# Attention scores computed from unsplit fp32 operands, with four smaller moves, in a one-core macaron block (RWKV-7 plus sliding-window attention)

## The chip, the core and the metric

The kernel runs on one core of a Trainium2 chip. The core has five engines that run side by side, each through its own list of instructions in order: TensorE (PE; its weight loads are listed as PEld), VectorE (DVE), ScalarE (ACT), GpSimd (POOL) and SyncE (SP), which here only issues DMAs. Matmuls write to PSUM; everything else lies in SBUF. The metric is the device time of one execution in microseconds, as the median of several runs.

## The reference, cut to what matters

One layer on x of 512 rows by 1024 columns, all in fp32:

```python
x = x + 0.5 * swiglu(rms_norm(x, norm_ffn1), ffn1_gate, ffn1_up, ffn1_down)   # 1024 -> 2816 -> 1024
p = rms_norm(x, norm_mix) @ w_in
o_rwkv = rwkv7_time_mix(p[..., :1792], ...)                 # 8 heads of 64, recurrent over rows
q, k, v = split(p[..., 1792:] + b_in_attn)                  # 8 query heads, 2 key/value heads of 64
scores = einsum('bnqhgd,bnkhd->bnhgqk', qb, kb) * 64 ** -0.5 # blocks of 128 rows, own and previous block
probs = softmax(concat([masked scores, sink]))[..., :-1]
out = einsum('bnhgqk,bnkhd->bnqhgd', probs, vb)
x = x + concat([o_rwkv, out]) @ w_out
x = x + 0.5 * swiglu(rms_norm(x, norm_ffn2), ffn2_gate, ffn2_up, ffn2_down)
return rms_norm(x, norm_final)
```

## The kernel before, in words

The program has five parts in a row: the first feed-forward net (`ffn("a")`), the input projections of the mixer, a joint stretch of recurrence and attention, the output projection (`out_mix`), and the second net (`ffn("b")`). In the nets and the projections PE issues matmuls without a pause to speak of. The large products are made in fp32r (names hi and lo): each operand is split into hi (rounded by ACT) and lo (the rest, by DVE), and three matmuls, hi·hi, lo·hi and hi·lo (`mm3w`, L683 to L685), give one product.

**Start.** `start` (L334) loads x in half rows (256 KB each) and the first weights over SP's queue: half row 0, the first two weight transfers (`a.loads(1)`), half rows 1 to 3, further weights. PE transposes each half row (xta), DVE scales it (xga), ACT and DVE split it (AaM).

**Plain stretch.** The last 256 hidden columns of a net are computed first, by `plain_step`, in four steps; at the fourth (L655) ACT and DVE make the results (gta, L658 and L659) and each is entered in the list `due`, with the step behind which PE transposes it (`hidden_turn`: hta on PE, hTa on ACT). Before, result t is due at step q + 1 + t, so the first transpose stands on PE behind the first of two X steps (L683 to L685, names Xa), 12 matmuls each.

**Join.** After the projections `join` (L1112) puts the inverse of the recurrence's triangle together: TT<-TB and held<-py on ACT and DVE, then on PE the product px, then TT<-px. The function `beside` puts other work between: the projection of v (`in_ps_av`), `split_k` and `split_q`, which make hi and lo of keys (ks, kl) and queries (qs), and the scores of unit 0. A unit is one block of 128 rows with one key/value head, four query heads; there are eight.

**Recurrence and attention.** What follows stands in a table written by hand (`ORDER`); its steps set the order on all engines. z is the product pz (eight matmuls) of a chunk, zd its copy by ACT (pack<-pz), u the product pu, sc the scores of a unit, m and w its maximum (DVE) and exponentials (ACT), t the transpose of the weights (pT) and te its copy (PT), a the product with v (av), wo the output projection. In `scores` (L1458) the two units of the first block multiply fp32 queries and keys directly, four matmuls over 64 rows and 128 columns. The six other units make two fp32r matmuls per head: queries' hi over lo, 128 rows deep, against ks, then queries' hi against kl, 64 rows deep, both with 256 columns. x, spilled to memory before, comes back by four DMAs that POOL issues (`unspill`, step ux); step var has POOL compute the power for a norm.

Of the kernel before, what the change touches and what calls it, by code (L numbers as in the profile page):

```python
# [53 lines left out]
gb.0 ud.2 s.2 w.4.1 m.6.0 o.2 a.2 n.2.0 oe.2 v.3 ah.2 we.4 te.3 n.2.1 z.3 m.6.1 wa.4.0 b.4 ve.3 al.2 sc.5 wd.4.1 zd.3  # L54
w.6.0 u.3 m.5.0 a.3 w.6.1 uv.3 t.4 m.5.1 ah.3 ud.3 s.3 we.6 te.4 al.3 o.3 n.3.0 sc.7 w.5.0 n.3.1 z.4 wa.6.0 m.7.0 b.5
w.5.1 wd.6.1 a.4 m.7.1 zd.4 t.6 oe.3 we.5 ah.4 wd.5.1 w.7.0 u.4 al.4 bp.1 uv.4 te.6 g.1 wd.5.0 w.7.1 bo.1 t.5 ud.4
we.7 s.4 wd.7.0 te.5 o.4 wd.7.1 a.6 oe.4 n.4.0 ge.1 a.5 n.4.1 ah.6 q.1 t.7 al.6 ah.5 b.6 wh.0 gb.1 z.5 al.5 te.7 var.1 ux
wl.0 q.0 a.7 zd.5 var.0 u.5 ah.7 wo.1.0 wh.1 al.7 uv.5 ns.1 s.5 ud.5 wl.1 ht.1 o.5 wo.1.1 n.5.0 oe.5 q.2 n.5.1 z.6 mg.1
b.7 wo.3.0 zd.6 var.2 xa.1 u.6 ns.0 wo.3.1 uv.6 ns.2 ud.6 s.6 xa.3 mh.1 o.6 n.6.0 ht.0 oe.6 ht.2 n.6.1 wo.0.0 mg.2 z.7
mg.0 mh.2 wo.0.1 zd.7 ml.2 mh.0 u.7 ml.1 wh.2 wo.2.0 xa.0 ud.7 wl.2 o.7 wo.2.1 oe.7 ml.0 q.3 wo.5.0 var.3 wh.3 xa.2  # L60
wl.3 wo.5.1 wo.4.0 xa.5 ns.3 wo.7.0 ht.3 wo.4.1 mg.3 wo.7.1 wh.4 xa.4 mh.3 wl.4 wo.6.0 ml.3 wo.6.1 xa.7 xa.6
# [121 lines left out]
class Net:  # L183
# [152 lines left out]
    def start(self, x):  # L336

        nc = self.nc
        self.warm()
        self.consts()  # L340
        xin = self.xin = self.new_rows()
        def load(h, *ts):
            for t in ts:
                nc.sync.dma_start(xin[t][:, h * S:h * S + S], x[0, t * P:(t + 1) * P, h * S:h * S + S])
        a = self.a = self.stream("a")
        load(0, 0)
        a.loads(1)
        load(0, 1, 2, 3)
        a.loads(2)
        load(1, 0, 1, 2, 3)  # L350
        a.loads(4)
        self.first_gain()
        self.ss = self.small("ss_a", 8, "ss")
        self.operands_begin("a")
        for t in range(2):
            self.start_turn(t, 0)
            if t == 0:
                a.split(0)
# [64 lines left out]
    def want_high(self, i):  # L423

        name, srcs = self.plan.pop(0)
        raw, n = self.weights_load(name, srcs)
        hi, lo = (self.wp.tile([P, 8, P], F32R, tag="o" + x, name=f"{x}_{name}", bufs=OUTW) for x in ("hi", "lo"))
        self.nc.scalar.activation(hi, raw, AF.Copy)
        self.half = name, raw, hi, lo

    def want_low(self, i):
        name, raw, hi, lo = self.half
# [13 lines left out]
    def weights(self, name, srcs):  # L446

        raw, n = self.weights_load(name, srcs)
        if name.startswith("be"):
            hi, lo = (self.tile4(f"{c}_{name}", (P, 8, P), F32R) for c in ("hi", "lo"))  # L450
        else:
            if name[0] == "o":
                hi, lo = (self.wp.tile([P, 8, P], F32R, tag="o" + x, name=f"{x}_{name}", bufs=OUTW) for x in ("hi", "lo"))
            else:
                hi, lo = (r.next(P) for r in self.split_rings)
        return self.weights_split(raw, n, hi, lo)
# [178 lines left out]
    def plain_step(self, st, pc):  # L635

        nc = self.nc
        if pc.idx == 0:
            self.banks["P"] = [self.acc(f"P{st.tag}{t}") for t in range(4)]
        bh, bl = st.parts[pc.q]  # L640
        for t in range(4):
            if pc.idx == 0 and t == 1 and st.tag == "a":
                for u in (2, 3):
                    self.operand_turn(self.xin[u], u, 0, self.gain1)
                for u in (2, 3):
                    self.operand_split(P_OPERANDS[1][0], u % 2)
            if pc.idx == 0 and t == 2 and st.tag == "b":
                self.out_turn(7)
            hi, lo = self.A[P_OPERANDS[t // 2][pc.idx // 2]]
            ts = slice(t % 2 * P, t % 2 * P + P)  # L650
            for j in range(2):
                k = 2 * (pc.idx % 2) + j
                self.mm3w(self.banks["P"][t], hi[:, k, ts], lo[:, k, ts], bh[:, j], bl[:, j], pc.idx == 0 and j == 0, pc.idx == 3 and j == 1)
        if pc.idx == 3:
            for t, b in enumerate(self.banks.pop("P")):  # L655
                ms = self.ms[:, t:t + 1]
                g, h = self.gt(f"pg{st.tag}{t}")[:, :256], self.gt(f"ph{st.tag}{t}")[:, :256]
                nc.scalar.activation(g, b[:, 256:], AF.Silu, scale=ms)  # L658
                nc.vector.scalar_tensor_tensor(h, b[:, :256], ms, g, ALU.mult, ALU.mult)  # L659
                self.due.append((pc.q + 1 + t, lambda t=t, h=h: self.hidden_turn(st, 5, t, h, 256)))  # L660

    def gu_step(self, st, pc):
        nc = self.nc
# [352 lines left out]
    def prep(self, p):  # L1016
        nc = self.nc
        k, r, a, Pd, Pi = self.kT[p], self.rT[p], self.icl[p], self.Pd[p], self.Pi[p]
        c3 = lambda t: t.rearrange("p (c t) -> p c t", c=NC)
        KR = self.KR[p] = self.tile4(f"KR{p}", (P, NC, 2, C))  # L1020
        BK = self.BK[p] = self.tile4(f"BK{p}", (P, NC, 2, C))
        STo = self.STo[p] = self.tile4(f"STo{p}", (P, NC, 2, C))
        kk = self.tile2(f"kk{p}")
        kk3 = c3(kk)
        nc.vector.scalar_tensor_tensor(kk, k, self.v("rwkv_k_k", p), self.knb[p].rearrange("p t s -> p (t s)"), ALU.mult, ALU.mult)
        nc.vector.tensor_tensor(KR[:, :, 1], c3(r), Pd, ALU.mult)
        nc.vector.tensor_tensor(KR[:, :, 0, 1:], kk3[:, :, 1:], Pd[:, :, :C - 1], ALU.mult)
        nc.vector.tensor_copy(KR[:, :, 0, 0], kk3[:, :, 0])
        nc.vector.tensor_tensor(kk, kk, a, ALU.mult)
        nc.scalar.activation(a, a, AF.Identity, scale=self.v("rwkv_k_a", p), bias=self.oka[:, p:p + 1])  # L1030
        nc.scalar.activation(STo[0:64], KR[64:128], AF.Copy)
        nc.vector.tensor_tensor(BK[:, :, 0], kk3, Pi, ALU.mult)
        nc.vector.tensor_tensor(k, k, a, ALU.mult)
        nc.vector.tensor_tensor(BK[:, :, 1], c3(k), Pi, ALU.mult)
# [124 lines left out]
    def gate(self, p):  # L1159

        nc = self.nc
        if p // 2 not in self.g:
            self.g[p // 2] = self.tile4(f"g{p // 2}")
        pt = self.gps[p] = self.psum(f"g_ps{p}")
        nc.tensor.matmul(pt, self.g2[:, p * P:(p + 1) * P], self.gl, start=True, stop=True)

# [7 lines left out]
    def mixer(self):  # L1174
# [55 lines left out]
        with self.tc.manual_schedule(engines=MAN):  # L1230
# [5 lines left out]
            def beside(i):  # L1236
                if i == 0:
                    part(0, 4)
                    self.split_k()
                    for n in range(1, 4):  # L1240
                        self.split_q(n)
                elif i == 1:
                    self.scores_all(0)
                    part(4, 8)
# [176 lines left out]
    def attn_begin(self):  # L1421
        nc = self.nc
        self.amix = self.pairs("am")
        self.sc, self.qs, self.PT, self.pp = {}, {}, {}, {}

    def attn_values(self):
        self.avn = self.psum("avn", (P, 4, P))
# [4 lines left out]
        self.Vn = self.keep("V", "Vn").rearrange("p (n c) -> p n c", n=4)  # L1432
        self.nc.scalar.activation(self.Vn, self.avn, AF.Copy)

    def split_k(self):

        nc = self.nc
        self.ks = self.x4.tile([P, 2, S], F32R, tag="ks", name="ks", bufs=1)
        self.kl = self.tile2("kl", dt=F32R) if "a" not in KEEP else self.t4.tile([P, 2, S], F32R, tag="kl", name="kl", bufs=1)[:, 0]
        for h in range(2):  # L1440
            r, o = (slice(x * 64, x * 64 + 64) for x in (h, 1 - h))
            nc.scalar.activation(self.ks[r, h], self.k[r], AF.Copy)
            nc.vector.tensor_tensor(self.kl[r], self.k[r], self.ks[r, h].bitcast(F32), ALU.subtract)
            nc.gpsimd.dma_start(self.ks[o, h], self.ks[r, h])

    def split_q(self, n):

        nc = self.nc
        qs = self.qs[n] = self.wp.tile([P, 2, 4, P], F32R, tag="qs", name=f"qs{n}", bufs=3)
        for i in range(2):  # L1450
            js = slice(2 * i, 2 * i + 2)
            for h in range(2):
                r, o = (slice(x * 64, x * 64 + 64) for x in (h, 1 - h))
                q, hi = self.q[i][r, :, n * P:(n + 1) * P], qs[r, h, js]
                nc.scalar.activation(hi, q, AF.Copy)
                nc.vector.tensor_tensor(qs[o, h, js], q, hi.bitcast(F32), ALU.subtract)

    def scores(self, u):  # L1458
        nc = self.nc
        n, h = u // 2, u % 2  # L1460
# [3 lines left out]
        pss = self.psum2(f"sc{u}", (P, 4, 2 * P))  # L1464
        for j in range(4):
            ks = slice((n - 1) * P + k0, (n + 1) * P)
            if n == 0:
                nc.tensor.matmul(pss[:, j, :W], self.q[j // 2][r0:r0 + 64, j % 2, :P], self.k[r0:r0 + 64, ks], start=True, stop=True)
            else:
                q = self.qs[n][:, h, j]  # L1470
                nc.tensor.matmul(pss[:, j, :W], q, self.ks[:, h, ks], start=True, stop=False)
                nc.tensor.matmul(pss[:, j, :W], q[r0:r0 + 64], self.kl[r0:r0 + 64, ks], start=False, stop=True)
        self.sc[u] = (self.extra4("sc", f"scs{u}", (P, 4, 2 * P)), W, pss) + tuple(self.small(f"{x}{u}", 4, x) for x in ("m", "nm", "es", "den"))

    def scores_max(self, u, half):
# [178 lines left out]
```

## Time and profile before

| | |
|---|---|
| median of 3 runs | 1001.09 us (999.86 to 1001.99) |
| profiled execution | 1002.43 us, its span 1000.7 us |
| PE busy | 976.9 us, 98% |
| DVE, ACT, POOL busy | 651.7, 502.9, 88.5 us |
| mean granted clock of PE | 0.988 |

The busy time of PE is modelled and contains the tail of each matmul, so 98% says that PE rarely stands, not that it works at its peak. A granted clock of 1.00 is 2.4 GHz, 0.50 is 1.2 GHz. The rows quoted below are of four kinds: sums of what PE waited for; busy time, clock and DMA share in chosen stretches; instructions in order of time (start in us, duration in us, engine, line, operation, output<-input, partitions x columns, count; in brackets the idle time of the engine before it and what ended it); and groups of equal instructions.

### The profile page before, as it was taken

How to read it: one execution, taken by the hardware profiler on the slowest of the kernel's cores; microseconds unless marked ns; L12 is line 12 of the kernel's file. 1: busy time of each engine (PE TensorE's matmuls, PEld its weight loads, DVE VectorE, ACT ScalarE, POOL GpSimd, SP SyncE). 2: the span in 40 equal slices, each digit the busy share in tenths (PEclk: the TensorE clock that was granted, in tenths of full speed). 3: DMA queues.
4: the chain of work that ended last, by engine and by line, in shares of the span. 5: the costliest groups of instructions: out<-in, count | busy, mean ns of one | idle time of the engine just before them, and what ended most of it. 6: DMA issues, size and time to landing. Idle time of an engine off the chain costs nothing.

```text
span 1000.7 us, 12967 instructions
## 1 busy us (share of the span) xinstructions
PE 976.9 (98%) x5041; PEld 794.6 (79%) x5041; DVE 651.7 (65%) x926; ACT 502.9 (50%) x777; POOL 88.5 (9%) x97
## 2 busy tenths in 40 slices
PE   8799999999999999999989999999999999999996
PEld 6688888888888886788876777887888888888885
DVE  5677667677522548699985687668767668753422
ACT  4655546546521327755466664265554654652302
POOL 0110010110000001120010030101010111000001
PEclk9899999999999999999999899999999999999999
DMA  9474855945332044223110253655594584533202
GB/s 316 106 168 113 225 135 122 232 105 182 111 104 84 12 103 140 75 74 73 43 33 23 52 152 132 226 156 147 124 234 110 143 202 97 206 126 115 75 1 84
DMA packets 83621, 124.09 MB, mean 124 GB/s; under 512 B 12772, under 2 KB 33320, under 8 KB 83560
## 3 DMA queue, kind: packets, MB, share of 16 engines
q1 hardware_dynamic: 67048, 89.17, 27.7%
q0 software_dynamic: 13856, 31.46, 15.8%
q10 hardware_dynamic: 2656, 2.63, 0.9%
q8 instruction: 39, 0.64, 0.3%
q14 instruction: 22, 0.18, 0.1%
HBM read 114.60 MB, written 6.29 MB: 121 GB/s over the span
## 4 chain that ended last, share of the span: by engine, by line
PE 85%; DVE 6%; ACT 4%; issue 2%; DMA 1%; POOL 1%; SPq 0%; POOLq 0%; ACTq 0%; DVEq 0%
PE da L685 4%; PE da L683 4%; PE db L685 4%; PE db L683 4%; PE da L684 4%; PE db L684 4%; PE Xa L685 4%; PE Xa L683 4%; PE Xa L684 4%; PE Xb L685 3%; PE Xb L683 3%; PE Xb L684 3%; PE Qb L685 2%; PE Qa L685 2%; PE Qa L683 2%
## 5 line engine op out<-in xcount | busy, mean ns | idle before, releaser
L160 ACT ACTIVATE hib<-rawa1b 128x1024 fp32r<-128x1024 f32 x38 | 40.2, 1057 | 58.4 <-PE db L684 19.4
L683 PE MATMUL da<-hia,dda 128*128 128x512 f32 x176 | 69.3, 394 | 0.0
L683 PE MATMUL db<-hib,ddb 128*128 128x512 f32 x176 | 68.8, 391 | 0.0
L685 PE MATMUL da<-loa,dda 128*128 128x512 f32 x176 | 68.6, 390 | 0.0
L684 PE MATMUL da<-hia,dda 128*128 128x512 f32 x176 | 68.5, 389 | 0.0
L685 PE MATMUL db<-lob,ddb 128*128 128x512 f32 x176 | 68.5, 389 | 0.0
L684 PE MATMUL db<-hib,ddb 128*128 128x512 f32 x176 | 68.5, 389 | 0.0
L160 ACT ACTIVATE hia<-rawa1a 128x1024 fp32r<-128x1024 f32 x38 | 40.1, 1055 | 49.6 <-DMA rawa1a<-in_ffn_gate_dram 17.6
L169 DVE TENSOR_TENSOR lob<-rawa1b,hib 128x1024 fp32r<-128x1024 f32 x38 | 46.4, 1220 | 28.3 <-PE db L685 22.6
L169 DVE TENSOR_TENSOR lob<-rawa0b,hib 128x1024 fp32r<-128x1024 f32 x38 | 46.4, 1220 | 28.3 <-PE db L685 21.7
L683 PE MATMUL Xa<-hia,AaM 128*128 128x512 f32 x160 | 64.0, 400 | 0.0
L685 PE MATMUL Xa<-loa,AaM 128*128 128x512 f32 x160 | 63.1, 395 | 0.9 <-DVE loa L169 0.9
L685 PE MATMUL Xb<-lob,AbM 128*128 128x512 f32 x160 | 62.6, 392 | 1.3 <-DVE lob L169 1.3
L683 PE MATMUL Xb<-hib,AbM 128*128 128x512 f32 x160 | 63.2, 395 | 0.0
L684 PE MATMUL Xa<-hia,AaM 128*128 128x512 f32 x160 | 62.8, 393 | 0.0
L684 PE MATMUL Xb<-hib,AbM 128*128 128x512 f32 x160 | 62.3, 390 | 0.0
L169 DVE TENSOR_TENSOR loa<-rawa0a,hia 128x1024 fp32r<-128x1024 f32 x38 | 46.4, 1220 | 20.9 <-PE da L685 14.6
L169 DVE TENSOR_TENSOR loa<-rawa1a,hia 128x1024 fp32r<-128x1024 f32 x38 | 46.4, 1220 | 15.8 <-PE da L685 8.8
L160 ACT ACTIVATE hib<-rawa0b 128x1024 fp32r<-128x1024 f32 x38 | 40.1, 1057 | 24.5 <-PE db L684 12.1
L160 ACT ACTIVATE hia<-rawa0a 128x1024 fp32r<-128x1024 f32 x38 | 40.1, 1055 | 15.4 <-PE da L684 11.2
L685 PEld LDWEIGHTS da<-loa,dda 128*128 128x128 f32 x176 | 33.0, 188 | 7.0
L685 PEld LDWEIGHTS db<-lob,ddb 128*128 128x128 f32 x176 | 33.0, 188 | 6.9
(460 smaller groups left out, 2527.9 us busy)
## 6 DMA issues: line engine op xcount, KB each, us to landing
rawa0a<-in_w_in_dram SPq DMA_DIRECT2D x16, 512.0 KB
rawa0a<-in_ffn_down_dram SPq DMA_DIRECT2D x11, 512.0 KB
rawa1a<-in_ffn_down_dram SPq DMA_DIRECT2D x11, 512.0 KB
rawa0b<-in_ffn_down_dram SPq DMA_DIRECT2D x11, 512.0 KB
rawa1b<-in_ffn_down_dram SPq DMA_DIRECT2D x11, 512.0 KB
rawba<-in_ffn_up_dram SPq DMA_DIRECT2D x10, 512.0 KB
rawba<-in_ffn_gate_dram SPq DMA_DIRECT2D x10, 512.0 KB
rawa0a<-in_ffn_gate_dram POOLq DMA_DIRECT2D x10, 512.0 KB, 5.9
```

Source lines behind the costliest of these rows:

```text
L160: self.nc.scalar.activation(hi, raw, AF.Copy)
L169: self.nc.vector.tensor_tensor(lo, raw, hi.bitcast(F32), ALU.subtract)
L683: mm(ps, ah, bh, start=first, stop=False, skip_group_check=True)
L684: mm(ps, al, bh, start=False, stop=False, skip_group_check=True)
L685: mm(ps, ah, bl, start=False, stop=last, skip_group_check=True)
```

## The change

1. **Scores.** `split_k` and `split_q` are gone. All eight units multiply the fp32 queries and keys: one matmul per head where two fp32r ones were. 
2. **Plain stretch.** Each transpose of a result is due one step later, in both nets. The eight result buffers are taken from their ring in another order, all gates first.
3. **First weights.** The first two weight transfers are issued from ACT's queue in place of SP's.
4. **Reload.** ux stands behind var.0 in the table in place of before it.
5. **Buffers.** KR and STo of a head pair, the two gate buffers, and hi and lo of each output weight each become one tile; the numbers of these buffers are as before or fall in with them, the first two move from one pool to another.

```diff
-we.7 s.4 ... al.5 te.7 var.1 ux
-wl.0 q.0 a.7 zd.5 var.0 u.5 ah.7 ...
+we.7 s.4 ... al.5 te.7 var.1
+wl.0 q.0 a.7 zd.5 var.0 ux u.5 ah.7 ...
...
-        a.loads(1)
+        a.loads(1, nc.scalar)
...
-        hi, lo = (self.wp.tile([P, 8, P], F32R, tag="o" + x, name=f"{x}_{name}", bufs=OUTW) for x in ("hi", "lo"))
+        hi, lo = self.out_pair(name)
...
+    def out_pair(self, name):
+        t = self.wp.tile([P, 2, 8, P], F32R, tag="ow", name="w_" + name, bufs=OUTW)
+        return t[:, 0], t[:, 1]
...
+            g4, h4 = ([self.gt(f"p{x}{st.tag}{t}")[:, :256] for t in range(4)] for x in "gh")
...
-                g, h = self.gt(f"pg{st.tag}{t}")[:, :256], self.gt(f"ph{st.tag}{t}")[:, :256]
+                g, h = g4[t], h4[t]
...
-                self.due.append((pc.q + 1 + t, lambda t=t, h=h: self.hidden_turn(st, 5, t, h, 256)))
+                self.due.append((pc.q + 2 + t, lambda t=t, h=h: self.hidden_turn(st, 5, t, h, 256)))
...
-        KR = self.KR[p] = self.tile4(f"KR{p}", (P, NC, 2, C))
-        STo = self.STo[p] = self.tile4(f"STo{p}", (P, NC, 2, C))
+        both = self.t8.tile([P, 2, NC, 2, C], F32, tag="KS", name=f"KS{p}", bufs=4)
+        KR, STo = self.KR[p], self.STo[p] = both[:, 0], both[:, 1]
...
-            self.g[p // 2] = self.tile4(f"g{p // 2}")
+            both = self.t8.tile([P, 2, 2, S], F32, tag="g", name="g", bufs=1)
+            self.g = {i: both[:, i] for i in range(2)}
...
                 if i == 0:
                     part(0, 4)
-                    self.split_k()
-                    for n in range(1, 4):
-                        self.split_q(n)
...
-            if n == 0:
-                nc.tensor.matmul(pss[:, j, :W], self.q[j // 2][r0:r0 + 64, j % 2, :P], self.k[r0:r0 + 64, ks], start=True, stop=True)
-            else:
-                q = self.qs[n][:, h, j]
-                nc.tensor.matmul(pss[:, j, :W], q, self.ks[:, h, ks], start=True, stop=False)
-                nc.tensor.matmul(pss[:, j, :W], q[r0:r0 + 64], self.kl[r0:r0 + 64, ks], start=False, stop=True)
+            nc.tensor.matmul(pss[:, j, :W], self.q[j // 2][r0:r0 + 64, j % 2, n * P:(n + 1) * P], self.k[r0:r0 + 64, ks], start=True, stop=True)
```

What this does to the lists of the engines is shown at three places. On ACT at the join, before; qs is the split of the queries for blocks 1 to 3, TT and held the moves of the join, held<-in_ps_av the copy of v, scs the exponentials:

```order
L1110 ACTIVATE TT<-TB 32x2x8x32 x4
L1110 ACTIVATE held<-py 128x256
L1442 ACTIVATE ks<-held 64x512 x2
L1455 ACTIVATE qs_3684<-q_2361 64x256 x2
L1455 ACTIVATE qs_3684<-q_2362 64x256 x2
L1455 ACTIVATE qs_3693<-q_2361 64x256 x2
L1455 ACTIVATE qs_3693<-q_2362 64x256 x2
L1455 ACTIVATE qs_3702<-q_2361 64x256 x2
L1455 ACTIVATE qs_3702<-q_2362 64x256 x2
L1110 ACTIVATE TT<-px 32x2x8x32 x2
L924 ACTIVATE held<-in_ps_av,pack_106 128x512
```

The same place on ACT in the changed kernel:

```order
L1115 ACTIVATE TT<-TB 32x2x8x32 x4
L1115 ACTIVATE held<-py 128x256
L1115 ACTIVATE TT<-px 32x2x8x32 x2
L929 ACTIVATE held<-in_ps_av,pack_106 128x512
L1466 ACTIVATE scs_3742,den_3746<-scs_3742,nm_3744 128x128 x4
```

The 14 instructions of the two splits are gone between held<-py and TT<-px; DVE loses the 14 that answer them.

On PE, one of the six units with 256 columns, before, between the product with v (av) and the transposes of v (pv):

```order
L1544 MATMUL av_3893<-PT_3874,held 64x256 x2
L1471 MATMUL sc_3898<-ks,qs_3684 128x256
L1472 MATMUL sc_3898<-kl,qs_3684 128x256
L1471 MATMUL sc_3898<-ks,qs_3684 128x256
L1472 MATMUL sc_3898<-kl,qs_3684 128x256
L1471 MATMUL sc_3898<-ks,qs_3684 128x256
L1472 MATMUL sc_3898<-kl,qs_3684 128x256
L1471 MATMUL sc_3898<-ks,qs_3684 128x256
L1472 MATMUL sc_3898<-kl,qs_3684 128x256
L1280 MATMUL pv_3919<-pack,held 128x128 x4
```

The same unit on PE in the changed kernel:

```order
L1519 MATMUL av_3854<-PT_3835,held 64x256 x2
L1447 MATMUL sc_3859<-held,q_2361 128x256 x2
L1447 MATMUL sc_3859<-held,q_2362 128x256 x2
L1283 MATMUL pv_3876<-pack,held 128x128 x4
```

Eight fp32r matmuls became four fp32 ones; the trace lists each fp32 matmul of this kind as two records.

On ACT behind the plain stretch of the first net, before; hTa is the copy of a transposed result, Xa_0 and Xa_1 the results of the two X steps, AaM an operand's hi:

```order
L160 ACTIVATE hia<-rawba 128x1024
L704 ACTIVATE gta<-Xa_0_367 128x512
L732 ACTIVATE hTa_381<-hta_0_382 128x2x128
L160 ACTIVATE hia<-rawa0a 128x1024
L572 ACTIVATE AaM_388<-xga_138 128x1024
L704 ACTIVATE gta<-Xa_1_391 128x512
L732 ACTIVATE hTa_381<-hta_1_405 128x2x128
```

The same place on ACT in the changed kernel:

```order
L160 ACTIVATE hia<-rawba 128x1024
L709 ACTIVATE gta<-Xa_0_367 128x512
L160 ACTIVATE hia<-rawa0a 128x1024
L576 ACTIVATE AaM_383<-xga_138 128x1024
L709 ACTIVATE gta<-Xa_1_386 128x512
L737 ACTIVATE hTa_400<-hta_0_401 128x2x128
L160 ACTIVATE hia<-rawa1a 128x1024
```

The copy of the first transpose moved behind the split of the operand and the copy of the second X step, as the transpose itself moved on PE behind the second X step.

## Rows read from the trace of the kernel before

**Rows 1.** What PE waited for: us in total, times, longest.

```profile
PE hta L731 <- DVE gta L659: 4.6, 1, 4.6
PE xta L536 <- DMA xN<-in_x_dram: 2.5, 1, 2.5
...
PE avn L1429 <- ACT held L924: 1.4, 1, 1.4
...
PE px L1134 <- ACT held L1110: 1.3, 1, 1.3
```

**Rows 2.** Stretches: length, busy PE, PEld, DVE, ACT, POOL, PE's clock, DMA.

```profile
522.18:529.00 6.82, 6.53 (x27) 3.72 (x28) 4.04 (x17) 3.72 (x11) 0.00 (x0) 0.50 0.01 2
559.72:563.14 3.42, 3.42 (x19) 2.44 (x18) 1.04 (x4) 3.18 (x11) 0.00 (x0) 1.00 0.01 2
563.14:566.55 3.41, 3.41 (x27) 2.10 (x27) 2.96 (x14) 1.06 (x7) 0.00 (x0) 0.50 0.00 0
...
573.38:576.79 3.41, 3.41 (x16) 2.18 (x16) 1.98 (x8) 2.70 (x8) 0.00 (x0) 0.50 0.98 306
576.79:588.00 11.21, 11.21 (x118) 8.58 (x116) 9.48 (x21) 9.84 (x24) 2.11 (x1) 1.00 0.03 11
```

**Rows 3.** In order of time, the issues of the first loads.

```profile
1.24 0.60 ACTq L243 DMA_DIRECT2D gain_rows<-in_norm_ffn_dram  x1
...
2.22 1.43 SPq L344 DMA_DIRECT2D xN<-in_x_dram  x3
```

**Rows 4.** In order of time, PE behind the plain stretch.

```profile
44.16 0.69 PE L731 MATMUL hta<-pack,gta 128*128 128x128 f32 x2 [4.60 <-DVE gta L659]
...
48.84 0.38 PE L731 MATMUL hta<-pack,gta 128*128 128x128 f32 x2
...
62.77 0.50 PE L685 MATMUL Xa<-loa,AaM 128*128 128x512 f32 x1 [0.31 <-DVE loa L169]
```

**Rows 5.** In order of time, ACT and DVE at the same place.

```profile
45.98 0.41 ACT L732 ACTIVATE hTa<-hta 128x256 f32<-128x256 f32 x1
...
48.31 1.22 DVE L573 TENSOR_TENSOR AaM<-xga,AaM 128x1024 fp32r<-128x1024 f32 x1 [0.76 <-ACT AaM L572]
```

**Rows 6.** In order of time, ACT at the join.

```profile
512.94 5.26 ACT L1455 ACTIVATE qs<-q 64x256 fp32r<-64x256 f32 x12
...
519.43 0.69 ACT L924 ACTIVATE held<-in_ps_av,pack 128x512 f32<-128x512 f32 x1
...
521.97 0.76 ACT L1322 ACTIVATE pack<-pz 64x256 f32<-64x256 f32 x2
```

**Rows 7.** In order of time, PE at the join.

```profile
516.84 0.33 PE L1317 MATMUL pz<-SU,KR 128*128 128x64 f32 x2
...
520.17 0.66 PE L1429 MATMUL avn<-pack,held 128*128 128x128 f32 x4 [1.44 <-ACT held L924]
...
522.47 1.44 PE L1328 MATMUL pu<-pack,TT 64*64 64x64 f32 x16 [0.56 <-ACT pack L1322]
```

**Rows 8.** In order of time, PE: a unit of scores, and what follows it.

```profile
530.60 0.38 PE L1471 MATMUL sc<-ks,qs 128*128 128x256 f32 x1
...
533.09 1.16 PE L1280 MATMUL pv<-pack,held 128*128 128x128 f32 x8
```

**Rows 9.** Groups on fp32 operands, 64 rows, 128 columns: busy us, mean ns.

```profile
L1048 PE MATMUL gram<-KR,BK 64*128 64x128 f32 x128 | 14.0, 278 | 0.0
...
L1468 PE MATMUL sc<-held,q 64*128 64x128 f32 x16 | 2.3, 285 | 0.0
```

**Rows 10.** In order of time, PE: eight records of one product at either clock.

```profile
573.27 1.91 PE L1544 MATMUL av<-PT,held 128*64 128x256 f32 x8
...
586.30 1.08 PE L1544 MATMUL av<-PT,held 128*64 128x256 f32 x8
```

**Rows 11.** In order of time, POOL at the reload.

```profile
588.36 2.21 POOL L887 DMA_DIRECT2D xN<-x_spill  x4
590.59 1.74 POOL L1376 TENSOR_TENSOR var<-var,pack 128x8 f32<-128x8 f32 x1
```

More of the change, by code (lines that the diff above doesn't have):

```diff
@@ L56 @@
 w.5.1 wd.6.1 a.4 m.7.1 zd.4 t.6 oe.3 we.5 ah.4 wd.5.1 w.7.0 u.4 al.4 bp.1 uv.4 te.6 g.1 wd.5.0 w.7.1 bo.1 t.5 ud.4
-we.7 s.4 wd.7.0 te.5 o.4 wd.7.1 a.6 oe.4 n.4.0 ge.1 a.5 n.4.1 ah.6 q.1 t.7 al.6 ah.5 b.6 wh.0 gb.1 z.5 al.5 te.7 var.1 ux
-wl.0 q.0 a.7 zd.5 var.0 u.5 ah.7 wo.1.0 wh.1 al.7 uv.5 ns.1 s.5 ud.5 wl.1 ht.1 o.5 wo.1.1 n.5.0 oe.5 q.2 n.5.1 z.6 mg.1
+we.7 s.4 wd.7.0 te.5 o.4 wd.7.1 a.6 oe.4 n.4.0 ge.1 a.5 n.4.1 ah.6 q.1 t.7 al.6 ah.5 b.6 wh.0 gb.1 z.5 al.5 te.7 var.1
+wl.0 q.0 a.7 zd.5 var.0 ux u.5 ah.7 wo.1.0 wh.1 al.7 uv.5 ns.1 s.5 ud.5 wl.1 ht.1 o.5 wo.1.1 n.5.0 oe.5 q.2 n.5.1 z.6 mg.1
 b.7 wo.3.0 zd.6 var.2 xa.1 u.6 ns.0 wo.3.1 uv.6 ns.2 ud.6 s.6 xa.3 mh.1 o.6 n.6.0 ht.0 oe.6 ht.2 n.6.1 wo.0.0 mg.2 z.7
@@ L452, in weights @@
             if name[0] == "o":
-                hi, lo = (self.wp.tile([P, 8, P], F32R, tag="o" + x, name=f"{x}_{name}", bufs=OUTW) for x in ("hi", "lo"))
+                hi, lo = self.out_pair(name)
             else:
@@ L1161, in gate @@
         nc = self.nc
-        if p // 2 not in self.g:
-            self.g[p // 2] = self.tile4(f"g{p // 2}")
+        if not self.g:
+            both = self.t8.tile([P, 2, 2, S], F32, tag="g", name="g", bufs=1)
+            self.g = {i: both[:, i] for i in range(2)}
         pt = self.gps[p] = self.psum(f"g_ps{p}")
@@ L1423, in attn_begin @@
         self.amix = self.pairs("am")
-        self.sc, self.qs, self.PT, self.pp = {}, {}, {}, {}
+        self.sc, self.PT, self.pp = {}, {}, {}
     def attn_values(self):
@@ L1433, in evac_vn @@
         self.nc.scalar.activation(self.Vn, self.avn, AF.Copy)
[L1435 to L1456, printed above, removed]
     def scores(self, u):
```

## The prediction

> **What bounds the kernel now.** I read first what PE waited for [rows 1], since PE is busy for nearly the whole span. The list is short: 4.6 us in front of the first transpose of a plain result, 2.5 us for the second half row of x at the start, 1.4 us and 1.3 us at the join. The reader is to see that few waits can be removed at all, so that a large gain has to come out of PE's own work or its clock. Next the stretches with the granted clock [rows 2]: at 522.18 to 529.00, 563.14 to 566.55 and 573.38 to 576.79 PE ran at 0.50, which is 1.2 GHz, all three in the stretch of recurrence and attention that the change touches. Ahead of the first it had stood twice at the join [rows 7]; ahead of the second it had not stood (3.42 of 3.42 busy) but issued a recurrence product and a unit of scores. Then the join and one unit of scores in order of time [rows 6 to 8].
>
> **The sum** is made against the profiled execution, 1002.43 us; it is 1.34 us over the median of the runs, 1001.09, and I take the sum's difference off the median.
>
> **Scores, the work itself.** Six units lose eight fp32r matmuls each and gain four fp32 ones. The old price is read directly: 530.60 to 533.09, 2.49 us [rows 8]. The new form, 64 rows and 256 columns in fp32, is not in the trace; two neighbours with 128 columns are. The gram product, long runs of it, takes 14.0 us for 128 records, 0.109 us each; the scores of the first block, in short runs, 2.3 us for 16, 0.144 us each [rows 9]. A unit will be eight records of twice the columns: 8 x 2 x 0.109 = 1.75 us at best, 8 x 2 x 0.144 = 2.30 us if all of the short run's excess grew with the columns. That excess is mostly the head and tail of a run, which do not double, so I take 1.88 us, near the lower end: 0.61 us less per unit, **3.7 us** in six. Bounds 6 x 0.19 = 1.1 us and 6 x 0.74 = 4.4 us. No wait covers any of this: PE stands in the list of waits at none of these units, so what a unit saves moves all that follows, as long as DVE and ACT keep up (below).
>
> **The splits at the join.** ACT loses 14 instructions; the 12 of the queries alone took 5.26 us [rows 6], and DVE loses 14 that ran beside them. Behind them on ACT stood the copy of v (519.43), then the exponentials and pack<-pz (521.97). PE waited for the first for 1.44 us and for the second for 0.56 us [rows 7]. PE leaves the projection of v at 516.84, where pz begins; without the splits the copy can start then and not at 519.43, 2.6 us earlier, and all of ACT behind it too. PE itself comes forward only by its two waits, 1.44 + 0.56 = **2.0 us**, and ACT stays ahead of it. What is late next is pu itself, the first matmul behind. Bounds: nothing (another operand of pu or avn late by as much) and 2.2 us. The 1.3 us that PE waits for held<-py in front of px [rows 1] end ahead of the splits, so they stay.
>
> **The clock.** If PE does not stand at 518.7 to 522.5, I expect it at full rate through what is now 522.18 to 529.00. How much that is worth is read from one product at both clocks: eight records of av took 1.91 us at half rate and 1.08 at full [rows 10], a saving of 43%. PE was busy there for 6.53 us [rows 2], so 0.43 x 6.53 = **2.8 us**; bounds 0 and half of it, 3.3 us. The two other half-rate stretches follow on scores. A score matmul of the old form comes every 2.49 / 8 = 0.31 us with 256 columns, slow for so few; the new records follow each other without such gaps. I expect both to go: 0.43 x (3.41 + 3.41) = **2.9 us**, bounds 0 and 3.4.
>
> **Plain stretch.** The transpose waits until 44.16 for DVE [rows 4], and nothing moves that moment. But 12 matmuls that stood behind the transpose now go ahead of it, into the wait: they took about 4.3 us between the two transposes at 44.16 and 48.84, at half rate, so up to 0.57 x 4.3 = 2.5 us. Little of it lasts: at 62.77 PE already waits for DVE's loa (0.31 us), and DVE runs a list of splits and sums from 48.31 on that does not depend on when PE is done. PE can gain only what DVE gains. That is the place of the copy hTa (0.41 us) on ACT, which leaves the front of the split that DVE waits for [rows 5]. **0.4 us**; bounds 0 and 2.5. In the second net PE has no such wait; there the move is worth nothing, since PE's matmuls hide it.
>
> **First weights.** Half row 1 was issued at 2.22, behind two weight transfers; at 1.43 us for three issues [rows 3] those two cost about 0.95 us, and by so much it is issued earlier. Against this the weights now stand behind ACT's own transfer, whose issue lasts until 1.84, and share the DMA engines with three half rows (1.43 us of issues). Bounds: 0.95 us gained, 1.4 us lost; I take **0.2 us** gained, since both first operands are needed within the same few microseconds. On ACT nothing waits behind the two issues: its first split comes long after.
> The Trainium skill speaks against this edit: "DMA: Bandwidth & Descriptors", section on queues, rings and completion order, says that each DMA engine takes turns between the queues by packet. By that the weights would fall back among the half rows, the wait for x would become one for weights, and this term would be 0, the sum 0.2 us smaller. No row here shows it.
>
> **Buffers and reload.** The joined buffers add no instruction; PE has no listed wait in the projections, where they reorder ACT and DVE, and I cost them at nothing; if that cover is gone it is a share of a microsecond. The reload is issued behind one more POOL power, 1.74 us [rows 11], and its readers on DVE come later by up to that; SP's and ACT's queues are not moved past.
>
> **What is given back.** Between 576.79 and 588 ACT is busy for 9.84 of 11.21 us and DVE for 9.48 [rows 2]. The work ahead of it shrinks on PE, not on ACT, so ACT has 1.37 us of slack to meet a PE that comes about 1.7 us sooner out of the last half-rate stretch. With the reload I take back **1.0 us**; bounds 0 and 1.37 + 1.74 = 3.1.
>
> Sum: 3.7 + 2.0 + 2.8 + 2.9 + 0.4 + 0.2 - 1.0 = 11.0 us. Profiled execution 991.4, median **990.1 us**.
>
> **The rivals.**
> *The clock still falls.* The wait in front of px stays, px has only 32-column blocks, and the recurrence's 64-column products stay between the scores. For it: clock falls at 563.14 without a wait of PE. Against it: the same wait in front of px is followed by no fall in this trace. If one of the two terms is lost, 2.8 or 2.9, the time is 993; if both, 995.8.
> *ACT takes PE's place.* The exponentials, copies and splits of 560 to 588 become the chain. For it: 9.84 of 11.21. Against it: PE's list has no wait for ACT there. It would eat the whole second clock term: 993.
> *The new scores are serial.* If an fp32 record could not begin before the one ahead of it ended, a record of 256 columns would take 0.278 us of its own [rows 9] plus 0.109 for the added columns, a unit 8 x 0.387 = 3.10 us, 0.61 us more than now, 3.7 us in six; PE would then stream less than now and both clock terms would go. With 2.0 + 0.4 + 0.2 gained and 1.0 given back: 2.1 us slower, 1003.2. It decides as soon as a unit costs more than 2.49 + 1.6 / 6 = 2.76 us. Against it: records of the same form follow each other every 0.109 us while each lasts 0.278.
> The Trainium skill has the rule by which this would come: "TensorE: Matmul & The Clock Gate", part on packing small matmuls, says that a weight load overlaps a running matmul only where their row groups differ, and the four heads of a unit use the same 64 rows. By that rule the result is this rival's. The gram rows, which also keep to one half of the rows for eight matmuls, contradict it.
> *Nothing arrives:* DVE and ACT hold the stretch anyway; about 1000.
>
> **How the numbers follow.** Forecast as summed, 62%: 990.1, own range 987 to 992.5. Clock falls once more 18%, 993 (both terms 3%, 995.8). ACT as the bound 8%. Better than the sum, with the plain stretch's 2.5 us or the gram price in full, 4%: 986 to 987. Nothing 2%, serial scores 3%. What a measurement of this kernel can tell from no change is about 0.2%, 2 us: faster by more 95%, within it 2%, slower by more 3%. The range 986 to 996 takes in the clock rivals and leaves out about one in ten.
>
> **What would show it.** In the profile of after: a unit of scores in 1.8 to 1.9 us; avn and pu without a wait; granted clock 1.00 from the join to the output projection; the wait in front of hta near 2 us with PE waiting for loa some 20 us later, now for longer; the first wait for x shorter. The prediction is wrong if a unit takes more than 2.3 us, if a half-rate stretch stays in the scores, or if new waits for ACT or DVE of more than 3 us stand between 520 and 620.

## The result and the profile after

The changed kernel takes 993.13 us, the median of 4 runs (992.78 to 993.54), against 1000.95 us for the kernel before in 4 runs (999.86 to 1001.99): a ratio of 0.9922, with a 95% interval from 0.9905 to 0.9939. So 7.8 us are gained; 11.0 were forecast. The profiled execution took 993.54 us, its span is 991.8 us.

From the page of the kernel after, the span and the busy time of each engine:

```profile
span 991.8 us, 12925 instructions
...
PE 968.0 (98%) x5041; PEld 790.7 (80%) x5041; DVE 644.7 (65%) x912; ACT 496.6 (50%) x763; POOL 87.3 (9%) x95
```

PE is busy 8.9 us less than before, and the span is 8.9 us shorter; the time that PE stood is the same in sum, but it stands elsewhere. What PE waited for in the kernel after (us in total, times, longest):

```profile
PE Pa L688 <- ACT hia L160: 5.5, 1, 5.5
PE hta L736 <- DVE gta L664: 1.8, 1, 1.8
...
PE Ya L690 <- DVE loa L169: 1.4, 1, 1.4
...
PE px L1139 <- ACT held L1115: 1.2, 1, 1.2
PE Qb L688 <- ACT hTb L737: 0.8, 1, 0.8
...
PE xta L540 <- DMA xN<-in_x_dram: 0.2, 1, 0.2
```

Against [rows 1], avn and pu are gone from the list, hta fell from 4.6 to 1.8 us and the wait for x from 2.5 to 0.2 us. The top line is new: the first matmul on weights stands 5.5 us for hia, the split of the weights whose transfers were moved to ACT's queue.

Stretches of the kernel after (length, busy time and matmuls of PE, granted clock, DMA share and GB/s):

```profile
8.00:18.20 10.20, 6.53 (x19) 0.50 1.04 366
...
512.00:518.83 6.83, 5.62 (x151) 1.00 0.34 79
518.83:525.65 6.82, 6.82 (x56) 1.00 0.01 2
...
560.00:566.80 6.80, 6.80 (x62) 1.00 0.01 4
566.80:573.70 6.90, 6.90 (x74) 1.00 0.61 184
```

The three half-rate stretches of [rows 2] have gone: PE runs at 1.00, which is 2.4 GHz, from the join on, in every stretch of 20 us from 500 to 620. A new one of 10.2 us at 1.2 GHz begins in the new wait at the start and outlasts it (PE issues matmuls in it from 11.64 on).

PE from the join to the end of the attention, in order of time (start, duration):

```profile
519.29 1.89 PE L1320 MATMUL pz<-SU,KS 128*128 128x64 f32 x16
...
521.02 0.61 PE L1432 MATMUL avn<-pack,held 128*128 128x128 f32 x4
...
522.64 0.68 PE L1331 MATMUL pu<-pack,TT 64*64 64x64 f32 x16
...
527.53 1.99 PE L1447 MATMUL sc<-held,q 64*128 64x256 f32 x8
529.45 1.16 PE L1283 MATMUL pv<-pack,held 128*128 128x128 f32 x8
...
577.29 1.08 PE L1519 MATMUL av<-PT,held 128*64 128x256 f32 x8
```

Subtract the same marks of before [rows 7, 8, 10]: pz comes 2.45 us later than before (519.29 against 516.84), pu 0.17 later, sc 3.07 earlier, pv 3.64 earlier, the last av 9.01 earlier. So the mixer gained 2.45 + 9.01 = 11.5 us in this pair of profiles, and PE entered it 2.45 us late. The loss lies ahead of it, and the experiments take both apart. From the first pz to the last av the mixer takes 58.0 us here (577.29 - 519.29) and 69.5 us before (586.30 - 516.84); this length is used below.

### The profile page after: what moved, and what is told of

Its sections match the earlier page's. It is cut to its first block, busy times and chain, and to the rows that moved or that the text cites. A ratio compares the mean times of both kernels' runs of the same rounds, so it can differ in the third digit from the quotient of the medians.

```text
span 991.8 us, 12925 instructions
## 1 busy us (share of the span) xinstructions
PE 968.0 (98%) x5041; PEld 790.7 (80%) x5041; DVE 644.7 (65%) x912; ACT 496.6 (50%) x763; POOL 87.3 (9%) x95
## 4 chain that ended last, share of the span: by engine, by line
PE 85%; DVE 8%; ACT 3%; issue 2%; DMA 1%; POOL 0%; POOLq 0%; ACTq 0%; SPq 0%; DVEq 0%
PE da L690 4%; PE da L689 4%; PE da L688 4%; PE db L688 4%; PE db L690 4%; PE db L689 4%; PE Xa L690 3%; PE Xb L690 3%; PE Xa L688 3%; PE Xb L688 3%; PE Xa L689 3%; PE Xb L689 3%; PE Qa L690 2%; PE Qb L688 2%; PE Qb L690 2%
## 5 line engine op out<-in xcount | busy, mean ns | idle before, releaser
L160 ACT ACTIVATE hia<-rawa0a 128x1024 fp32r<-128x1024 f32 x38 | 40.1, 1056 | 19.8 <-PE da L689 11.2
```

## Experiments

Each is compared with runs of the kernel before on the same chip; medians of those were 1001.35, 999.53 and 1001.25 us in the three groups of runs.

### The first weights, taken back alone and added alone

after_spw is the changed kernel with this line as before:

```diff
-        a.loads(1, nc.scalar)
+        a.loads(1)
```

> The changed kernel, with the two first weight transfers back on SP's queue, between half row 0 and half row 1 of x; nothing else. Theory 'start': the 2.5 to 3.7 us by which TensorE's marks stand later behind the start of the changed kernel (the first Pa 2.56 us, the transposes of the plain results 2.96 us) come from these two transfers alone, and what is behind the plain stretch keeps 2.5 us of it to the end: 990.6 us, the wait of Pa for hia (5.5 us) gone, the wait of xta for x back at about 2.5 us, no half-rate stretch between 8 and 18 us. Rival 'absorbed': DVE's list of splits and sums in the plain stretch holds TensorE there whatever the start does, and the late marks come from the turn that was moved: 992.5 to 993.5.

Measured: 989.79 us (989.46 to 990.45), ratio 0.9899 (0.9881 to 0.9918). "Start" holds, with 0.8 us more gained than it said; only the half-rate stretch that was to be gone between 8 and 18 us is shorter and not gone (mean clock 0.83 from 8 to 18.2, 0.50 in the changed kernel). In place of the 5.5 us for hia, PE's list begins with

```profile
PE xta L540 <- DMA xN<-in_x_dram: 2.2, 1, 2.2
```

before_wact is the kernel before with the opposite edit.

> The kernel before, with the two first weight transfers on ACT's queue; nothing else. Theory 'start': they fall back among the half rows of x, hia comes 3 us later, TensorE's clock falls to half behind that wait, and 2.5 us are lost for good: 1003.5 us. Rival 'absorbed': the wait of 4.6 us in front of hta takes it up: 1001 us.

Measured: 1003.96 us (1000.24 to 1006.67), ratio 1.0029 (1.0014 to 1.0045). Its list begins:

```profile
PE Pa L683 <- ACT hia L160: 5.5, 1, 5.5
PE hta L731 <- DVE gta L659: 4.6, 1, 4.6
```

The edit costs 3.3 us in the one pair (993.13 - 989.79; 2.3 us by the two ratios, since the medians come from different groups of runs) and 2.6 us in the other (95% interval 1.4 to 4.5), and it brings the wait of 5.5 us with it each time. The rival falls: the wait in front of hta stands at 4.6 us in spite of a late start, because what it waits for is late too (DVE makes gta at 45.98 in before_wact, at 43.62 before). How the loss comes about is seen in the kernel after, ACT's issues and the readers in order of time:

```profile
1.86 0.40 ACTq L145 DMA_DIRECT2D rawa0a<-in_ffn_up_dram  x1
...
2.29 0.48 ACTq L145 DMA_DIRECT2D rawa0a<-in_ffn_gate_dram  x1
...
10.53 1.06 ACT L160 ACTIVATE hia<-rawa0a 128x1024 fp32r<-128x1024 f32 x1 [3.81 <-DMA rawa0a<-in_ffn_gate_dram]
...
11.64 0.80 PE L688 MATMUL Pa<-hia,AaM 128*128 128x512 f32 x1 [5.47 <-ACT hia L160]
```

The second transfer is issued at 2.29 and read at 10.53, 8.2 us later. Between 3 and 4.5 us the queues of the kernel after (q1 is SP's, q10 ACT's; packets, MB, share of the 16 engines' time) show

```profile
q1 hardware_dynamic: 212, 0.38, 72.7%
q10 hardware_dynamic: 4, 0.00, 0.8%
```

and from 6 to 7.5 us

```profile
q1 hardware_dynamic: 202, 0.29, 52.8%
q10 hardware_dynamic: 268, 0.26, 50.4%
```

From 4.5 us on (36.8% and 30.1% from there to 6) both queues are served in the same stretches, with shares not far from equal. "DMA: Bandwidth & Descriptors" of the Trainium skill, section on queues, rings and completion order, says that each DMA engine takes turns between queues by packet; the trace agrees in so far as both queues move data side by side, and doesn't show whether they alternate by packet. Turns alone don't account for the delay: up to 4.5 us ACT's queue had moved next to nothing of two transfers issued at 1.86 and 2.29. In that stretch, 3 to 4.5 us, the two shares add up to 73.5% here, 82% in before_wact and 86% in after_x1act (below), while the eleven kernels with all of this on SP's queue have 93.6 to 105.3%. Why ACT's queue starts so late is not settled.

### The scores, with and without the splits

before_sc is the kernel before with unsplit scores and no splits; before_sck keeps the splits at the join, unread.

```diff
+            nc.tensor.matmul(pss[:, j, :W], self.q[j // 2][r0:r0 + 64, j % 2, n * P:(n + 1) * P], self.k[r0:r0 + 64, ks], start=True, stop=True)
-            if n == 0:
...
-                nc.tensor.matmul(pss[:, j, :W], q[r0:r0 + 64], self.kl[r0:r0 + 64, ks], start=False, stop=True)
```

and in before_sc alone

```diff
-                    self.split_k()
-                    for n in range(1, 4):
-                        self.split_q(n)
```

> The kernel before, with the unsplit scores and without the splits of keys and queries; first weights, turn, buffers and reload as before. Theory 'mixer': this edit alone carries the whole gain, units of 1.92 us instead of 2.49 (3.4 us in six), two waits at the join (2.0 us), three half-rate stretches (5.7 us): 11 us, 990 us. Rival 'buffers': some 2 us of the gain behind the join come from the joined buffers and the later reload, 992.

Measured: 991.09 us (990.10 to 991.74), ratio 0.9910 (0.9893 to 0.9927). "Mixer" holds: the mixer takes 57.99 us (573.69 - 515.70) with the old buffers and the old reload, 58.00 us in the changed kernel. So "buffers" falls. spw_noturn (below), which differs from before_sc only in the buffers, their order and the reload, has 991.17 us.

> The kernel before with the unsplit scores, but the splits of keys and queries still made at the join, on ACT, DVE and POOL's queue, and read by nobody. Theory 'two places': TensorE still waits at avn and pu (1.44 + 0.56 us) and still runs at half rate from 522 to 529, but not at 563 and 573: 3.4 us of score work and 2.9 us of clock, 995 us. Rival 'one place': the scores alone set the clock, the stretch behind the join is at full rate too: 992. Rival 'no scores': the clock at 563 and 573 falls as before, because it follows on the join: 997.5.

Measured: 996.01 us (995.03 to 997.28), ratio 0.9960 (0.9947 to 0.9972). PE at the join of before_sck, in order of time:

```profile
519.31 0.66 PE L1429 MATMUL avn<-pack,held 128*128 128x128 f32 x4 [1.46 <-ACT held L924]
...
521.91 1.44 PE L1328 MATMUL pu<-pack,TT 64*64 64x64 f32 x16 [0.86 <-ACT pack L1322]
```

and three stretches of it (columns as above):

```profile
521.00:527.80 6.80, 5.94 (x25) 0.50 0.01 2
527.80:562.00 34.20, 34.20 (x287) 1.00 0.14 32
562.00:578.00 16.00, 16.00 (x152) 1.00 0.26 83
```

"Two places" holds by the rows, and both rivals fall: with the splits' waits the clock falls behind the join, and with the new scores it doesn't fall later. The same goes for every profile taken: the nine kernels with the new scores have no half-rate stretch between 530 and 640 us, the five with the old ones have two or three each. The splits at the join with their half-rate stretch cost 996.01 - 991.09 = 4.9 us (by the mixers' lengths, 63.55 and 57.99, 5.6); the score work and the later clock 1001.35 - 996.01 = 5.3 us by the medians, 4.0 by the ratio (2.8 to 5.3).

before_late is the other way round: old scores, but two thirds of the queries' splits moved behind the join.

```diff
-                    for n in range(1, 4):
-                        self.split_q(n)
+                    self.split_q(1)
+... sq="split_q", ...
-... wd.2.0 te.1 o.1 ... g.0 zd.2 m.4.0 ...
+... wd.2.0 te.1 sq.2 o.1 ... g.0 zd.2 sq.3 m.4.0 ...
```

> The kernel before with its split scores; only the splits of the queries of blocks 2 and 3 leave the join and are made just ahead of the units that read them; those of the keys and of block 1 stay. ACT has then eight splits (about 3.5 us) less ahead of the copy of v. Theory 'two places': avn and pu no longer wait (2.0 us), TensorE runs at full rate behind the join (2.8 us), the half-rate stretches near 563 and 573 stay: 996.5 us, somewhat more if the late splits hold ACT up between 540 and 560. Rival 'old scores set the clock everywhere': the stretch behind the join stays at half rate: 999.3.

Measured: 998.51 us (994.55 to 998.98), ratio 0.9984 (0.9972 to 0.9996). Its stretches, and a new line in its list of waits:

```profile
515.00:523.00 8.00, 8.00 (x61) 1.00 0.01 2
523.00:531.00 8.00, 8.00 (x62) 1.00 0.08 19
546.10:549.50 3.40, 3.40 (x23) 0.50 0.00 0
559.70:563.10 3.40, 3.40 (x27) 0.50 0.34 77
570.00:573.40 3.40, 3.40 (x16) 0.50 0.97 298
```

```profile
PE pz L1316 <- ACT scs L1490: 0.8, 1, 0.8
```

avn and pu don't wait, and PE runs at 2.4 GHz behind the join, as expected; the time is 2 us above the 996.5 expected, and against its own group of runs the gain is 1.0 us by the medians and 1.6 by the ratio (0.4 to 2.8), where 4.8 were expected. A part of the gain is given back: 0.8 us waiting for ACT, which now makes the late splits, and a third short half-rate stretch at 546.1. The median of before is itself uncertain here, as the next kernel shows.

before_again is the kernel before, unchanged.

> The kernel before, unchanged, to see what separates its runs near 998 us from those near 1002 us, which have the same code. Theory 'clock': they differ in which of the half-rate stretches behind the join are there, by 1.4 us for a short one of 3.4 us and 2.8 us for a long one of 6.8 us; a run near 998 lacks the long one behind the join or has it as a short one. Rival 'start': they differ in when the first half rows of x land.

Measured: 1000.91 us (999.20 to 1001.92), its profiled span 999.0 us against 1000.7 in the first profile. Its stretches:

```profile
522.20:525.60 3.40, 3.29 (x19) 0.50 0.00 0
525.60:529.00 3.40, 3.40 (x36) 0.99 0.03 5
549.50:552.90 3.40, 3.40 (x25) 0.50 0.00 0
563.20:566.60 3.40, 3.40 (x28) 0.50 0.00 0
566.60:580.00 13.40, 13.40 (x124) 1.00 0.41 119
```

Against [rows 2], the stretch behind the join is half as long, the one at 573 is missing, and there is one at 549.5. These are 3.4 us less at half rate, worth 0.43 x 3.4 = 1.5 of the 1.7 us between the two spans, while PE enters the mixer only 0.14 us sooner (516.70 against 516.84): that speaks for "clock" and against "start", though no run near 998 us was profiled. The same code meets half rate at other places from run to run; with it the runs of before spread over 5 us (997.58 to 1002.58 in 23 runs of one group), while those of after_spw lie within 1 us.

### The late turn

before_turn is the kernel before with the late turn and the new order of the result buffers:

```diff
+            g4, h4 = ...
...
-                self.due.append((pc.q + 1 + t, ...
+                self.due.append((pc.q + 2 + t, ...
```

> The kernel before with only the turn of the plain results one step later, in both nets. Theory 'DVE's list holds the stretch': the wait in front of hta falls from 4.6 to 1.9 us, but a wait for loa of 1.4 us and half-rate time come back behind it: 0.4 to 1.3 us, 1000.0 to 1001.0. Rival 'in full': 2.5 us, 998.8. Rival 'lost in the second net', where Qb now waits 0.8 us for hTb: 1001.3 to 1002.

Measured: 999.10 us (996.74 to 1001.08), ratio 0.9993 (0.9980 to 1.0006): too wide to tell the three apart. (Its profile has a half-rate stretch from 512.3 to 515, behind the wait in front of px, and none from 522 to 529, where avn doesn't wait: the fall that the prediction looked for behind px does come in one run.) So the turn was also taken back where the runs lie closer together, spw_noturn.

> The changed kernel with the first weights back on SP and the turn of the plain results back to one step earlier, in both nets. Theory 'the turn is worth what the marks show': the wait in front of hta is 4.6 us again, and the later waits for loa (1.4 us) and hTb (0.8 us) go; 0.5 to 1.3 us slower than with the late turn: 990.3 to 991.1 us, against 989.8. Rival 'in full': 2.5 us, 992.3. Rival 'nothing': 989.8.

Measured: 991.17 us (990.36 to 991.46) against 989.79 (989.46 to 990.45) with the late turn; one profile of each puts the difference of the spans at 0.7 us (988.7 against 988.0). PE behind the plain stretch of after_spw, and then of spw_noturn, in order of time:

```profile
43.25 0.44 PE L736 MATMUL hta<-pack,gta 128*128 128x128 f32 x2 [1.88 <-DVE gta L664]
45.56 0.50 PE L690 MATMUL Ya<-loa,AaM 128*128 128x512 f32 x1 [1.40 <-DVE loa L169]
...
61.41 0.50 PE L690 MATMUL Xa<-loa,AaM 128*128 128x512 f32 x1 [0.73 <-DVE loa L169]
```

```profile
43.30 0.69 PE L736 MATMUL hta<-pack,gta 128*128 128x128 f32 x2 [4.57 <-DVE gta L664]
...
61.75 0.50 PE L690 MATMUL Xa<-loa,AaM 128*128 128x512 f32 x1 [0.39 <-DVE loa L169]
```

The wait in front of hta is 2.7 us shorter, and 18 us later PE meets the matmul on the same split loa only 61.75 - 61.41 = 0.34 us sooner: DVE's list sets that moment. "In full" falls.

### The reload

spw_ux puts ux back in front of var.0 in after_spw.

```diff
-te.7 var.1 ... var.0 ux u.5
+te.7 var.1 ux ... var.0 u.5
```

> The changed kernel with the first weights back on SP and the reload of the spilled rows back in its old place, ahead of the power var.0. Theory: TensorE has no wait between 560 and 620 us in the changed kernel, so nothing is given back there, by the reload or by ACT's crowd: 989.8 us. Rival 'the reload costs what the forecast took back': the old place is 0.5 to 1.0 us faster, 988.8 to 989.3.

Measured: 990.63 us (989.48 to 990.73). The old place isn't faster, and the mixer takes 58.01 us (573.96 - 515.95), as in the changed kernel; the forecast's price for it has nothing to stand on. In the same group of runs spw_noturn is 0.5 us above this kernel.

### Towards a faster kernel

after_x1act sends half row 1 of x over ACT's queue, with the weights on SP.

```diff
-        load(0, 1, 2, 3)
+        nc.scalar.dma_start(xin[1][:, :S], x[0, P:2 * P, :S])
+        load(0, 2, 3)
```

> The changed kernel with the first weights back on SP and half row 1 of x by ACT's queue in their stead. Theory 'turns by packet': half row 1 is a quarter of a megabyte, the weights are half of one, so it lands earlier than behind the weights; the wait of xta for x (2.2 us) goes, hia and loa of the first weights come next and are late by 0.5 to 1.5 us: 988.5 to 989.5 us, against 989.8 with all of it on SP. Rival 'whatever ACT's queue carries lands late': 990 to 992, the wait for x longer than 2.2 us.

Measured: 991.35 us (991.08 to 991.55), 1.6 us above after_spw (in another group of runs). From its start, in order of time:

```profile
1.87 0.37 ACTq L348 DMA_DIRECT2D xN<-in_x_dram  x1
...
8.29 0.88 PE L541 MATMUL xta<-pack,xN 128*128 128x128 f32 x4 [2.73 <-DMA xN<-in_x_dram]
8.36 1.06 ACT L160 ACTIVATE hia<-rawa0a 128x1024 fp32r<-128x1024 f32 x1 [1.40 <-DMA rawa0a<-in_ffn_gate_dram]
```

The forecast for this run failed, its rival holds: a quarter of a megabyte, issued 0.35 us earlier than in [rows 3], is read at 8.29, no earlier than the 7.76 of after_spw, and the weights, issued on SP at the same moment as before, are late as well.

after_eb is after_spw with the two copies of py ahead of the moves of TB in the join.

```diff
+        for gq in range(2):
+            self.move(gq, self.EB[:, gq], py[:, gq * 8:gq * 8 + 8], 1.0)
         for q, b in enumerate(blocks):
...
-        for gq in range(2):
-            self.move(gq, self.EB[:, gq], py[:, gq * 8:gq * 8 + 8], 1.0)
```

> The changed kernel with the first weights back on SP, and at the join the two copies of py into EB, for which px waits 1.3 us, ahead of the eight moves of TB into TT on ACT and DVE. Theory: px starts as soon as the projection of v's first half is done, 1.3 us earlier, and nothing reads TT before pu, 8 us later: 988.5 us. Rival: the moves of TT, later by 0.4 us on each engine, and the copies behind them hold zd or pu up: 989.8. What also counts is the clock, which is at full rate in spite of the wait: no gain there.

Measured: 989.18 us (988.87 to 989.42), ratio 0.9902 (0.9884 to 0.9920). px no longer waits, and the span falls from 988.0 to 987.1 us; by the medians the gain over after_spw is 0.6 us, about the spread of the runs: no clear gain. best also takes the late turn back in the second net.

> The changed kernel with the first weights on SP, the two copies of py into EB ahead of the moves into TT, and the late turn in the first net alone. Theory: Qb's wait of 0.8 us for hTb goes with the early turn in the second net, where the wait in front of the transposes was nothing: 988.4 us, against 989.2 with the late turn in both. Rival: the transposes in the second net then wait for DVE as in the first: 989.2 or more.

Measured: 989.42 us (988.86 to 989.62). No gain: in place of 0.8 us for hTb, PE waits in the second net for lob, as the rival said in another form.

```profile
PE Xb L690 <- DVE lob L169: 1.2, 2, 0.7
```

So the fastest kernel here is the changed one with the first weights back on SP and, if anything, the copies of py first: 989.2 us, 4 us under the changed kernel.

## Why the prediction was right in the mixer and wrong at the start

The time, 993.13 us, is 3.0 us above the forecast of 990.1 and lies in the range. It equals the time of the rival "clock still falls", 993, for another reason: in the mixer the clock does not fall. That the time lies in the range is luck in part: the range was widened for the rivals on the clock, and what used it is the first weights, whose own bounds (0.95 us gained, 1.4 lost) don't hold the loss measured.

| step | forecast | measured | from |
|---|---|---|---|
| score work | -3.7 | -3.4 | six units at 1.92 us |
| splits at the join, and the clock behind it | -4.8 | -4.9 to -5.6 | before_sck to before_sc, medians and mixers |
| two later half-rate stretches | -2.9 | -0.6 to -1.9 | before to before_sck, ratio and medians, less the score work |
| plain stretch | -0.4 | -0.5 to -1.4 | spw_noturn to spw_ux and to after_spw |
| first weights | -0.2 | +2.3 to +3.3 | after_spw to after, ratios and medians |
| given back | +1.0 | 0 | spw_ux, waits of after, mixers |

**Scores.** Right. The unit takes 529.45 - 527.53 = 1.92 us at full rate, where 1.88 was taken between 1.75 and 2.30. The group in the kernel after, in order line, engine, operation, count, busy us and mean ns:

```profile
L1447 PE MATMUL sc<-held,q 64*128 64x256 f32 x48 | 11.9, 390 | 0.0
```

A record lasts 0.390 us, and eight follow each other in 1.92 us, 0.24 apart. The rival "serial" is out. So is, for this form, the rule of the Trainium skill that would have brought it ("TensorE: Matmul & The Clock Gate", part on packing small matmuls): a unit's eight weight loads last 0.187 us each and use the same rows, and 0.24 us from record to record would leave 0.05 us for 256 columns if no load overlapped a matmul, half of the 0.109 us in which records of 128 columns follow each other [rows 9]. The same part of that page also names a background buffer that a load may go to; no run here tells whether that is the way.

**Join and clock.** Right in size and in mechanism: what before_sck keeps is what the step named, and its 4.9 us are the 2.0 and 2.8 of the sum. That the two later stretches follow on the form of the scores is shown by before_sck, which has neither, and by before_late, which keeps such stretches without a wait at the join; why the old form brings them is not shown. Their size, 2.9, was read from one profile. before_again shows that they move from run to run, so the term is one outcome of several, and too large for the runs: 4.0 - 3.4 = 0.6 us by the ratio, at most 5.3 - 3.4 = 1.9.

**Plain stretch.** Right: DVE's list holds it. The wait for loa came where it was looked for (0.73 us, 18 us later in after_spw) and also earlier, 1.40 us at the first Ya. In the second net the move is worth about nothing, as was said, but not because PE has no wait there: before, PE waited 1.3 us for lob, after, 0.3 us for lob and 0.8 us for hTb.

**First weights.** This step failed, in sign and size. It priced the delay of the weights by the time that three issues take, 1.43 us [rows 3], as if a transfer were late by as much as its issue stands behind others. Rows of before had a better price, in order of time:

```profile
7.11 1.04 ACT L160 ACTIVATE hia<-rawa0a 128x1024 fp32r<-128x1024 f32 x1
...
8.31 1.11 PE L536 MATMUL xta<-pack,xN 128*128 128x128 f32 x4 [2.50 <-DMA xN<-in_x_dram]
...
9.08 0.78 PE L683 MATMUL Pa<-hia,AaM 128*128 128x512 f32 x1
```

Half row 1 was issued at 2.22 [rows 3] and PE waited for it until 8.31, 6.1 us. The second weight transfer, issued at 2.29, had to be expected about as late, at 2.29 + 6.1 = 8.4 us, and the first product on it 1.1 us behind, at 9.5, against 9.08 before: 0.4 us lost in place of 0.2 gained. That gives the sign and not the size. The measured 10.53 is 2.1 us later still: ACT's queue moved next to nothing up to 4.5 us and shared the engines with SP's from there. The first product comes at 11.64, 2.56 us later than before. A second part of the cost is the clock: from this product to the first on the next operand, the same 12 products and 8 transposes take 7.02 us in the kernel after (to 18.66), 5.86 before and 5.67 in after_spw, as PE runs at 1.2 GHz up to 18.2 us. The wait for x did get shorter, 2.5 to 0.2 us, as the prediction had asked for; it only was no longer the last. The prediction had written down that the wait for x would become one for weights, and had put even that at nothing.

**Given back.** ACT's crowd and the reload cost nothing: no wait of PE in the kernel after stands between the join and the output projection, and the mixer takes 57.99 to 58.01 us in all eight kernels with the new scores and no splits, with the reload early or late. In the pair of profiles on which the sum was made the mixer gained 11.5 us, where 3.7 + 2.0 + 2.8 + 2.9 = 11.4 stood before the 1.0 us was taken back. That the size fits so well belongs to that profile: against the mixer of before_again, 67.9 us (584.58 - 516.70), the gain is 9.9 us, and before_sc, the mixer's edit alone, gains 10.3 us by the medians and 9.0 by the ratio (7.3 to 10.7).

## What to carry to other kernels

Where operands are only 64 rows deep, one fp32 matmul can beat two rounded ones (here 0.48 against 0.62 us per head), and leaving out the splits can be worth more than the matmuls: price the work, the waits that the splits cause, and the clock behind them apart. A transfer that is moved to another queue is not priced by how long issues take; even the 6.1 us that its neighbours took from issue to reader were too few here (8.2). A small edit that rides along with a large one deserves a run of its own: here it gave away about three of eleven microseconds, and the total looked like a plausible rival.

## What was not expected of the hardware

With transfers issued on SP's and ACT's queues, the 16 DMA engines were busy for less of the time from 3 to 4.5 us (73.5% in the kernel after, 82% in before_wact, 86% in after_x1act) than in the eleven kernels with all of it on SP's queue (93.6 to 105.3%, as the profile adds up the packets' time), and ACT's queue had 0.8, 5.6 and 11.2% of it, though its transfers had been issued by 2.3 us. From 4.5 to 6 us the number of queues no longer tells the kernels apart: 67, 87 and 67% with two, anything from 62% (before_late) to 100.5% (after_spw) with one. And half-rate stretches of one program differ from run to run in place and number, behind the same waits and the same matmuls: the mixer of the kernel before took 69.5 and 67.9 us in two profiles, while in the eight profiles without such stretches it took 57.99 to 58.01. The row of the clock can miss such a stretch: in the first profile of before it says 1.00 from 8 to 18.2 us, while the first products there stand 0.43 us apart, as they do at 0.50 in the kernel after, and 0.23 apart later.
